# Four column groups of w_in as seven half-width products in a stage of their own

## The chip, the cores and the metric

The kernel runs on one core of a Trainium2 chip. The metric is the time of one execution in microseconds (us) on the device. The profiler takes one execution more, and the trace and its page are of that one.

## What is computed

One block of a network on x of 512 tokens by 2048 features, all in float32: a norm, the projection by `w_in`, eight heads of sparse attention (NSA, in two key groups) beside four heads of retention, the projection by `w_out`, and a feed-forward part with squared ReLU. Cut to what matters:

```python
h = rms_norm(x, norm_mix_pre)                       # 512 x 2048
proj = h @ w_in                                     # 2048 x 6680
q_a, kv_a, gate_a, q_r, k_r, v_r, g_r = split(proj) # 1024, 6*256, 24, then 4 times 1024
k_cmp = compress_kv(kv6[0], ...); v_cmp = compress_kv(kv6[1], ...)   # a small MLP over 31 windows of 32 tokens
gates = sigmoid(gate_a)
o_a = nsa_attention(q_a, k_cmp, v_cmp, kv6[2], ..., kv6[5], gates, t5_bias)
q_r, k_r = rope(q_r), rope(k_r)
o_r = silu(g_r) * retention(q_r, k_r, v_r)          # per head of 256, chunks of 128
mix = concat([o_a, o_r]) @ w_out
x = x + rms_norm(mix, norm_mix_post)
u = square(relu(rms_norm(x, norm_mlp_pre) @ w_up))  # 2048 x 8192
x = x + rms_norm(u @ w_down, norm_mlp_post)
```

With 512 tokens every block of keys is among the chosen and the window reaches over all of them, so the chosen keys and the window keys are each all keys up to the token.

## The kernel before, in words

**Products.** Each float32 product is three matmuls on rounded halves (`mm3`, L155 to L157): `split` (L141) makes the high half by an ACT cast (L143) and the low half by a DVE subtraction (L144). The normed and transposed x is kept as `Hh`, `Hl`. A weight *slab* is 256 rows of `w_in` by up to 512 columns (`Slab`, L168); SP's queue loads it into `raw`, `split` makes `whi`, `wlo`. A column group is eight slabs, one *block* of steps (B = 8). `feat_major` (L202) puts features on the partitions, `tok_major` (L224) tokens; both issue per slab 24 matmuls of the group's width (512 columns; 256 for v's second group), 192 to a group.

**Order.** `Driver` `drv` (L267) walks the steps: kv, k, q0 (512 columns each), v1 (256), then for each retention head `qk` and `vg` (512 each), with q1 behind head 0's. `Side` (L67) holds the units that run between: the bias table, two `compress` units, 16 `nsa_unit`s (group g, query tile i, pair of heads), four `ret_unit`s. A unit has a first part (scores) and a second (mixing, `outs`). A pump after each piece of a step (6 matmuls) lets one step of each part go: `two` at every second piece, `three` at three pieces of four, and `side.drain(units, firsts)` issues what is left until so many units are through. All of this is fixed when the program is made: each engine then takes its instructions in that order.

**The units' chains.** `nsa_unit`: scores on PE (L584), scaled and biased by DVE (L585), maxima (L603, L608), six exponentials on ACT (L612), a reciprocal and scalings on DVE (L616 to L622), four transposes per key tile (L647) whose results are split into `ph`, `pl`, and mixing matmuls into the bank `oT`, of which there is one. `ret_unit`'s `outs` (L713): for query tile i, i+1 matmuls into `oT` (L742), statistics by DVE (L744, L745, L161), a power by POOL (L162), two DVE passes (L748, L749), and the next tile's gate (ACT L717, DVE L718 to L720).

**The front.** x's norm and transposes run beside v0 with the gates (280 columns, `tok_outer`). Then the driver begins.

**After retention**: `w_out` (416 columns at a time, beside ret_unit 3), then up and down, which already use seven products for eight (`Feed`, from L893): of two halves of the rows and two of the columns, sums of weight quarters (DVE adds) times sums of x quarters, 256 columns to a matmul in up. These are left as they are.

Of the kernel before, what the change touches and what calls it, by code (L numbers as in the profile page):

```python
# [112 lines left out]
def block_kernel(ctx: ExitStack, tc: tile.TileContext, x, norm_mix_pre, w_in, cmp_pe_k, cmp_w1_k, cmp_b1_k,  # L113
# [54 lines left out]
    class Slab:  # L168
# [11 lines left out]
        def load(self):  # L180
# [4 lines left out]
            hi = pool.tile([P, KC, width], F32R, name="whi")  # L185
            lo = pool.tile([P, KC, width], F32R, name="wlo")
# [77 lines left out]

    side = Side()
# [36 lines left out]
    gw.tile([P, 16], F32, name="gap_w")  # L302
    wp = wctx.enter_context(tc.tile_pool(name="wp", bufs=3, side="right"))
    pool_a = lambda: (wp, S)
    actx, rctx = ExitStack(), ExitStack()
    ap = actx.enter_context(tc.tile_pool(name="att", bufs=1))


    def x_load(t, q):
        if q == 0:  # L310
            xts[t] = ap.tile([P, DM], F32, name="xt", tag="P", bufs=2)
# [4 lines left out]
    ones = ap.tile([1, P], F32, name="ones")  # L316
# [4 lines left out]
    g1 = ap.tile([1, DM], F32, name="g1", tag="P", bufs=2)  # L321
# [4 lines left out]
    gb = ap.tile([P, DM], F32, name="gb", tag="big")  # L326
# [15 lines left out]
    def x_square(t, q):  # L342
        if q == 0:
            hx[t] = ap.tile([P, DM if t % 2 else NG * 32 + DM], F32, name="h", tag="qT" if t % 2 else "kT")
            sx[t] = ap.tile([P, 8], F32, name="st", bufs=2)
        c = slice(q * 512, (q + 1) * 512)
        nc.scalar.activation(hx[t][:, c], xts[t][:, c], AF.Square, accum_out=sx[t][:, q:q + 1])
# [9 lines left out]
    Vh = ap.tile([P, NT, 2, NG * DK], F32R, name="Vh")  # L357
    Vl = ap.tile([P, NT, 2, NG * DK], F32R, name="Vl")
    gat = ap.tile([P, NT, 3 * HA], F32, name="gat")

    def v_done(b):
        def done(t, ps):
# [3 lines left out]
            split(Vh[:, t, b, :], Vl[:, t, b, :], ps[:, :NG * DK])  # L366
# [9 lines left out]
    ep = ectx.enter_context(tc.tile_pool(name="early", bufs=NSLAB))  # L376
    v0 = slabs_of(w_in, [(OFF_KV + 768, NG * DK), (OFF_GATE, 3 * HA)], lambda: (ep, NG * DK + 3 * HA))
    first = tok_outer(v0, NG * DK + 3 * HA, v_done(0))
    kv0 = slabs_of(w_in, [(OFF_KV, 512)], pool_a)
# [9 lines left out]
    for i in range(3, NSLAB):  # L389
        v0[i].fetch(wp.tile([P, KC, S], F32, name="raw", tag="whi" if i % 2 else "wlo"))  # L390
        if i in (3, 4):
            x_load(1, i - 1)
# [11 lines left out]
    for n in range(4 * NT):  # L404
# [20 lines left out]
        if n == 3:  # L425
            kv0[0].fetch()
            kv0[1].fetch()
        if n in (7, 11):
            kv0[n // 11].load()
# [4 lines left out]
    for _ in products:  # L434
        pass
    ectx.close()
    rp = rctx.enter_context(tc.tile_pool(name="ret", bufs=1, side="right", reuse_waits="tile"))

    hot = ap.tile([33, 640], F32, name="hot", tag="P", bufs=2)
    nc.gpsimd.dma_start(hot, c_hot)
    tbl = ap.tile([33, HA], F32, name="tbl")
    nc.vector.memset(tbl[32:33, :], NEG)
    nc.gpsimd.dma_start(tbl[0:32, :], t5_bias)
    g3r = ap.tile([KT, P], F32, name="g3r")
    nc.gpsimd.dma_start(g3r, norm_mlp_pre.rearrange("o (k p) -> (o k) p", p=P))
    rot = rp.tile([P, 2, S], F32, name="rot")
    nc.gpsimd.dma_start(rot, c_rot)
    RB = 16  # L450
    rd = dram.tile([HA, RB, RD], F32, name="rd")

    def bias_table():
        rsb = ap.tile([HA, 640], F32, name="rsb", tag="P", bufs=2)
        for c0, n in ((0, 512), (512, 128)):
            ps = bank("S")
            nc.tensor.matmul(ps[:HA, :n], tbl, hot[:, c0:c0 + n], start=True, stop=True)
            nc.vector.tensor_copy(rsb[:, c0:c0 + n], ps[:HA, :n])
            yield
        nc.gpsimd.dma_start(rd, rsb[:, None, :].to_broadcast([HA, RB, RD]))  # L460
        pt = bank("PT", 2)
        nc.tensor.transpose(pt[:, :KT], g3r, ident[:KT, :KT])
        nc.vector.tensor_copy(g3T, pt[:, :KT])
        yield

# [12 lines left out]
    def kv_done(f, ps):  # L478
        if f % 2 == 0:
            KV[f // 2] = ap.tile([P, NG * S + CBLK], F32, name="KV", tag="P", bufs=2)  # L480
        nc.scalar.copy(KV[f // 2][:, f % 2 * S:(f % 2 + 1) * S], ps)

    def compress(i):
        pe, w1, b1, w2 = ((cmp_pe_k, cmp_w1_k, cmp_b1_k, cmp_w2_k), (cmp_pe_v, cmp_w1_v, cmp_b1_v, cmp_w2_v))[i]
        kv = KV[i]
        pes = ap.tile([CBLK, DK], F32, name="pes")
        nc.sync.dma_start(pes, pe[0])
        b1s = ap.tile([DK, 2], F32, name="b1s")
        nc.sync.dma_start(b1s[:, 0:1], b1.rearrange("o n -> n o"))
        w2s = ap.tile([DK, DK], F32, name="w2s")  # L490
        nc.sync.dma_start(w2s, w2[0])
        w1s = [ap.tile([P, 16, DK], F32, name="w1s", tag=("qT", "big")[c]) for c in range(2)]
        for c in range(2):
            nc.sync.dma_start(w1s[c], w1[0][c * 16 * P:(c + 1) * 16 * P, :].rearrange("(l p) n -> p l n", p=P))
            yield
# [5 lines left out]
        for l in range(CBLK):  # L501
            nc.tensor.matmul(hid[:65, :DK], kv[:, l:l + STRIDE * 64 + 1:STRIDE], w1s[l // 16][:, l % 16, :],  # L502
                             start=l == 0, stop=l == CBLK - 1)
            if l % 8 == 7:
                yield
        hs = ap.tile([65, DK], F32, name="hs")
        nc.scalar.copy(hs, hid[:65, :DK])
        yield
# [3 lines left out]
        z = ap.tile([DK, 4, 63], F32, name="z")  # L512
# [25 lines left out]
    def k_done(f, ps):  # L538
        nc.scalar.copy(kW[:, f % 2, :] if f // 2 else kS[:, f % 2, 32:], ps)

    def q_done(g):
        def done(f, ps):
            if f == 0:
                QT[g] = ap.tile([P, 4, S], F32, name="qT", tag="qT")
            nc.scalar.copy(QT[g][:, f, :], ps)
        return done
# [10 lines left out]
    def nsa_unit(g, i, pr):  # L557
# [7 lines left out]
        def scores():  # L565
# [196 lines left out]
    def proj(cols, done, tok=False):  # L762
        sl = slabs_of(w_in, cols, pool_a)
# [783 lines left out]
```

## Time and profile before

| what | us |
|---|---|
| three timed runs: median (lowest to highest) | 2201.61 (2201.35 to 2202.2) |
| the profiled execution: its time, its span | 2200.95, 2199.0 |
| PE busy, of 12787 matmul rows | 2154.7 (98%) |
| PEld (weight loads) | 1910.5 (87%) |
| DVE | 1535.1 (70%) |
| ACT | 984.4 (45%) |
| POOL | 122.7 (6%) |
| mean granted TensorE clock | 0.994 |

The busy time of PE is the sum of modelled spans that overlap; how fast it goes is read from the start of one matmul to the start of the next. Share of the chain that ended last: PE 90%, DVE 5%, the rest 1% each or less.

### The profile page before, as it was taken

The page shows a single profiled execution, that of the slowest core. Times are in us where ns is not written, and L with a number is a line of the kernel's source. Part 1 is how long each engine was busy: PE and PEld are TensorE (multiplying, and loading weights), DVE is VectorE, ACT ScalarE, POOL GpSimd, SP SyncE. Part 2 cuts the span into 40 slices and gives each one's busy share as a digit, 9 for nine tenths or more (in the row PEclk, how much of TensorE's full clock was granted, in tenths as well). Part 3 has the DMA queues.
Part 4 walks back from the last instruction along what each step waited for, and adds up shares of the span by engine and source line. Part 5 has one row for each costly group of instructions (what it writes and reads, how often), then busy time and mean ns, then how long its engine had stood idle before and what let it go on. Part 6 is the DMA issues. An engine that isn't in the chain of part 4 may idle for free.

```text
span 2199.0 us, 31984 instructions
## 1 busy us (share of the span) xinstructions
PE 2154.7 (98%) x12787; PEld 1910.5 (87%) x12787; DVE 1535.1 (70%) x1828; ACT 984.4 (45%) x1425; POOL 122.7 (6%) x139
## 2 busy tenths in 40 slices
PE   8999999999999999999999999999999999999995
PEld 7888878878788899999999999999888888888874
DVE  6213555554555533578988877777878999999996
ACT  5213343343232323485554555555664454445453
POOL 0000000000000000000000000000000000000011
PEclk9999999999999999999999999999999999999997
DMA  6543324322324334577877757676775757566684
GB/s 198 135 120 90 94 65 96 94 75 82 86 75 124 109 101 129 176 233 214 230 218 205 207 165 204 168 205 184 235 230 166 213 157 224 145 202 185 189 220 99
DMA packets 255462, 348.97 MB, mean 159 GB/s; under 512 B 16299, under 2 KB 166139, under 8 KB 254417
## 3 DMA queue, kind: packets, MB, share of 16 engines
q1 hardware_dynamic: 199472, 263.07, 38.0%
q0 software_dynamic: 29616, 42.96, 11.8%
q10 hardware_dynamic: 26226, 40.91, 5.1%
q8 instruction: 100, 1.64, 0.3%
q14 instruction: 48, 0.39, 0.1%
HBM read 305.14 MB, written 41.75 MB: 158 GB/s over the span
## 4 chain that ended last, share of the span: by engine, by line
PE 90%; DVE 5%; issue 1%; ACT 1%; DMA 1%; POOL 0%; SPq 0%; DVEq 0%; ACTq 0%; POOLq 0%
PE prod L157 17%; PE prod L155 17%; PE prod L156 17%; PE mm L155 11%; PE mm L157 11%; PE mm L156 11%; PE S L584 2%; DVE wlo L938 2%; PE PT L647 1%; PE S L707 1%; PE oT L742 1%; PE oT L502 1%; PE oT L155 1%; PE oT L156 1%; PE oT L157 1%
## 5 line engine op out<-in xcount | busy, mean ns | idle before, releaser
L961 ACT CAST whi<-Y 128x1024 fp32r<-128x1024 f32 x227 | 238.2, 1050 | 283.1 <-PE prod L157 117.6
L156 PE MATMUL prod<-wlo,Hh 128*128 128x512 f32 x896 | 349.4, 390 | 2.3 <-DVE wlo L938 2.1
L157 PE MATMUL prod<-whi,Hl 128*128 128x512 f32 x896 | 348.7, 389 | 0.0
L155 PE MATMUL prod<-whi,Hh 128*128 128x512 f32 x896 | 348.6, 389 | 0.0
L144 DVE TENSOR_TENSOR wlo<-raw,whi 128x1024 fp32r<-128x1024 f32 (+4 forms) x152 | 168.6, 1113 | 255.1 <-ACT whi L143 254.6
L961 ACT CAST whi<-low 128x1024 fp32r<-128x1024 f32 x215 | 226.4, 1054 | 265.1 <-PE prod L157 131.6
L938 DVE TENSOR_TENSOR wlo<-Y,whi 128x1024 fp32r<-128x1024 f32 x227 | 276.8, 1220 | 51.5 <-ACT whi L961 50.5
L938 DVE TENSOR_TENSOR wlo<-low,whi 128x1024 fp32r<-128x1024 f32 x215 | 262.1, 1221 | 55.9 <-ACT whi L961 55.0
L157 PE MATMUL prod<-Hh,wlo 128*128 128x256 f32 x1024 | 284.3, 278 | 5.1 <-DVE wlo L938 5.1
L155 PE MATMUL prod<-Hh,whi 128*128 128x256 f32 x1024 | 284.6, 278 | 0.3 <-ACT Hh L143 0.3
L156 PE MATMUL prod<-Hl,whi 128*128 128x256 f32 x1024 | 284.0, 277 | 0.9 <-DVE Hl L144 0.9
L143 ACT CAST whi<-raw 128x1024 fp32r<-128x1024 f32 (+4 forms) x152 | 145.6, 960 | 302.0 <-PE mm L156 147.9
L155 PE MATMUL mm<-whi,Hh 128*128 128x416 f32 (+4 forms) x704 | 262.3, 373 | 0.6 <-ACT Hh L143 0.5
L157 PE MATMUL mm<-whi,Hl 128*128 128x416 f32 (+4 forms) x704 | 248.1, 352 | 0.7 <-DVE Hl L144 0.7
L156 PE MATMUL mm<-wlo,Hh 128*128 128x416 f32 (+4 forms) x704 | 247.6, 352 | 0.0
L155 PE MATMUL mm<-Hh,whi 128*128 128x512 f32 x512 | 214.7, 419 | 0.1
L155 PE MATMUL prod<-sx,whi 128*128 128x256 f32 x768 | 212.0, 276 | 0.0
L156 PE MATMUL prod<-sx,whi 128*128 128x256 f32 x768 | 212.0, 276 | 0.0
L157 PE MATMUL prod<-sx,wlo 128*128 128x256 f32 x768 | 212.0, 276 | 0.0
L156 PEld LDWEIGHTS prod<-wlo,Hh 128*128 128x128 f32 x896 | 168.2, 188 | 40.1 <-DVE wlo L938 5.3
L157 PE MATMUL mm<-Hh,wlo 128*128 128x512 f32 x512 | 200.5, 392 | 0.0
L156 PE MATMUL mm<-Hl,whi 128*128 128x512 f32 x512 | 200.0, 391 | 0.0
(273 smaller groups left out, 3909.4 us busy)
## 6 DMA issues: line engine op xcount, KB each, us to landing
raw<-in_w_in SPq DMA_DIRECT2D x160, 256.0 KB, 3.1
low<-in_w_up SPq DMA_DIRECT2D x76, 512.0 KB, 4.3
Y<-in_w_up SPq DMA_DIRECT2D x64, 512.0 KB, 4.7
low<-in_w_down SPq DMA_DIRECT2D x64, 512.0 KB, 4.6
Y<-in_w_down SPq DMA_DIRECT2D x64, 512.0 KB, 4.6
Y<-ud SPq DMA_DIRECT2D x49, 512.0 KB, 8.0
ud<-Y ACTq DMA_DIRECT2D x77, 256.0 KB, 4.8
raw<-in_w_out SPq DMA_DIRECT2D x32, 416.0 KB, 3.5
```

The source lines that it names most:

```text
L143: nc.scalar.copy(hi, src)
L144: nc.vector.tensor_sub(lo, src, hi.bitcast(F32))
L155: nc.tensor.matmul(ps, ah, bh, start=first, stop=False, skip_group_check=more)
L156: nc.tensor.matmul(ps, ah, bl, start=False, stop=False, skip_group_check=more)
L157: nc.tensor.matmul(ps, al, bh, start=False, stop=last, skip_group_check=more)
L502: nc.tensor.matmul(hid[:65, :DK], kv[:, l:l + STRIDE * 64 + 1:STRIDE], w1s[l // 16][:, l % 16, :], start=l == 0, stop=l == CBLK - 1)
L584: nc.tensor.matmul(sps[:, :c + L], QT[g][:, h, qs], k, start=True, stop=True)
L647: nc.tensor.transpose(pt[:, e * P:(e + 1) * P], Pt[:, e, rows_of(j)], ident)
L707: nc.tensor.matmul(sps[:, :n], QK[:, 2 + d, rows_of(j)], QK[:, d, j * P:], start=d == 0, stop=d == 1)
L742: nc.tensor.matmul(o[:, :DR], AT[:, a0:a0 + P], vr[:, j, :], start=j == 0, stop=j == i)
L938: nc.vector.tensor_sub(lo, src, hi.bitcast(F32))
L961: nc.scalar.copy(hi, src)
```

## The change

Four groups of 512 columns (kv, k, q0, q1: `INC`) are no longer products of 512 columns under the driver. They are made by `groups()` in a stage of their own between v and retention: for each group seven products of 48 matmuls of 256 columns, 336 in all, where 192 of 512 columns stood; the scheme is that of up. `Feed` and `Later` are moved up and take their pool and place as arguments. The steps:

- v1 is the driver's first block. Beside it, `in_sums()` makes the four sums of x quarters that the products need (28 DVE operations of 128x1024, 8 ACT casts; each second piece of a step, and later each second piece of `groups()`). Three weight operands are made (`ifeed.advance()`) two steps before v1 ends.
- `in_done` takes a product's bank to `z[0]`, `z[1]` by ACT or DVE; ACT's queue stores them to `pd` in DRAM (512 KB each). v's halves go to `vd` in DRAM by POOL's queue; v1's results lie two to a buffer (`vst`).
- POOL's queue loads them back, and the compressor's weights: kv and the first compressor's at the end of `groups()`, the second's during the first compressor, V (2 MB) at the second's middle, then k, the bias `BT` (8 transfers), q0; q1 later.
- The bias table is made in one piece behind v0's products; its three loads are issued by POOL at n == 9 of x's norm.
- The eight retention blocks are now blocks 2 to 9 of the driver (v1 is the first); side units go beside the first seven. ret 0 stands ahead of i = 2 of group 0, ret 2 ahead of i = 2 of group 1; `every` pumps after each piece.

```diff
-    kv0 = slabs_of(w_in, [(OFF_KV, 512)], pool_a)
+    first = tok_outer(v0, NG * DK + 3 * HA, v_done(0, lambda: xp.tile([P, S], F32R, name='vst')))
+    v1 = slabs_of(w_in, [(OFF_KV + 1280, 256)], pool_a)
...
     def v_done(b, vst):
-            split(Vh[:, t, b, :], Vl[:, t, b, :], ps[:, :NG * DK])
+            v = vst().rearrange("p (a n) -> p a n", a=2)
+            split(v[:, 0, :], v[:, 1, :], ps[:, :NG * DK])
+            nc.gpsimd.dma_start(vd[:, :, t, b, :].rearrange("a p n -> p a n"), v)
...
+    INC = [(OFF_KV, OFF_KV + 256), (OFF_KV + 512, OFF_KV + 1024), (0, 256), (512, 768)]
...
+    def groups():
+        for i, (g, p, _) in enumerate(iphases):
...
+                ps = mm.tile([P, S], F32, name="mm")
...
+            for s in range(2):
+                hi, lo = ifeed.slab()
+                if s == 0 and sets:
+                    in_done(*sets.pop())
...
+                for f in range(2):
+                    for kk in range(4):
+                        k = 4 * s + kk
+                        o = ps[:, f * 256:(f + 1) * 256]
...
+                        mm3(o, hi[:, kk, rows_of(f)], lo[:, kk, rows_of(f)], xh[:, k, :], xl[:, k, :], start, last,
+                            more)
+                    yield
...
+    drv.steps += tok_major(v1, 256, v_done(1, vst))
+    work = in_sums()
+    sums = lambda c: next(work, None) if c % 2 else None
...
+    drv.run(len(drv.steps) - 2, pump=sums)
+    raws = [wr.tile([P, KC, S], F32, name="raw").rearrange("p k n -> p (k n)") for _ in range(3)]
+    ifeed.free += raws
+    for _ in range(3):
+        ifeed.advance()
+    drv.run(len(drv.steps) - 1, pump=sums)
+    drv.run()
+    next_up = slabs_of(w_in, [(OFF_QR, DR), (OFF_KR, DR)], pool_a)
+    for n, _ in enumerate(groups()):
+        if n % 2 or n % 8 == 0:
+            next(work, None)
...
-            nc.sync.dma_start(w1s[c], w1[0][c * 16 * P:(c + 1) * 16 * P, :].rearrange("(l p) n -> p l n", p=P))
+            nc.gpsimd.dma_start(w1s[c], w1[0][c * 16 * P:(c + 1) * 16 * P, :].rearrange("(l p) n -> p l n", p=P))
...
+    def loads():
+        k_load()
+        load_bias(0)
+        q_load(0)
+        for _ in range(6):
+            yield
...
+    side.add(lambda: compress(0), nothing)
+    side.add(lambda: compress(1), nothing)
+    side.add(loads, nothing)
     for u in range(8):
-        side.add(*nsa_unit(0, u // 2, u % 2), after(3), after(4))
-    side.add(*ret_unit(0), after(6))
+        if u == 4:
+            side.add(*ret_unit(0), after(2), after(3))
+        side.add(*nsa_unit(0, u // 2, u % 2))
+    side.add(*ret_unit(1), after(4), after(5))
     for u in range(8):
-        side.add(*nsa_unit(1, u // 2, u % 2), after(7))
-        if u == 5:
-            side.add(*ret_unit(1), after(9))
-    side.add(*ret_unit(2), after(10), after(11))
-    side.add(*ret_unit(3), after(12))
-    for blocks, units, firsts, pump in ((3, 3, 0, two), (4, 0, 0, two), (7, 10, 11, three), (8, 11, 12, three),
-                                        (9, 12, 12, three), (10, 12, 19, two), (11, 19, 19, two),
-                                        (12, 22, 22, three)):
+        if u == 4:
+            side.add(*ret_unit(2), after(6), after(7))
+        side.add(*nsa_unit(1, u // 2, u % 2))
+    side.add(*ret_unit(3), after(8))
+    kv_load()
+    compress_load(0)
+    for blocks, units, firsts, pump in ((2, 0, 0, every), (3, 0, 0, three), (4, 7, 8, three), (5, 8, 0, three),
+                                        (6, 12, 13, three), (7, 13, 0, three), (8, 22, 22, every)):
         drv.run(blocks * B - 1, pump=pump)
         side.drain(units, firsts)
```

**Where v1 ends and the groups begin, ACT, in the changed kernel** (`half_`: a loaded quarter of weights; `sv_`: a sum of x quarters; `da`: a result; L143 splits `whi` and `vst`, L362 is the cast in `Feed.advance`, L656 the one in `in_sums`):

```order
L143 CAST whi<-raw 128x2x256 x4
L656 CAST sv_613<-db 128x1024 x2
L143 CAST whi<-raw 128x2x256 x2
L362 CAST whi<-half_621 128x1024
L362 CAST whi<-half_622 128x1024
L362 CAST whi<-half_623 128x1024
L656 CAST sv_617<-db 128x1024 x2
L143 CAST vst<-mm 128x256 x4
L362 CAST whi<-half_624 128x1024
L362 CAST whi<-half_625 128x1024
L681 COPY da<-mm 128x2x256
```

And DVE at the same place:

```order
L339 TENSOR_TENSOR wlo<-half_621,whi 128x1024
L339 TENSOR_TENSOR wlo<-half_622,whi 128x1024
L658 TENSOR_TENSOR sv_618<-db,sv_617 128x1024 x2
L144 TENSOR_TENSOR vst<-mm,vst 128x256 x4
L644 TENSOR_TENSOR db<-db,Hh 128x1024 x2
```

The third weight cast and the two of a sum stand ahead of v1's casts on ACT, and the sum's two subtractions ahead of v1's on DVE; none of these rows is in the kernel before.

**The outs of retention head 2, DVE, before** (`rst` statistics, `rn` the normed result, `sg`, `gr` the gate):

```order
L719 RECIPROCAL sg<-sg 128x256
L720 TENSOR_TENSOR gr<-gr,sg 128x256
L144 TENSOR_TENSOR wlo<-raw,whi 128x1024
L744 BN_STATS rst<-oT 128x6
L745 BN_AGGR rst<-rst 128x2
L161 TENSOR_SCALAR rst<-rst 128x1
L748 TENSOR_SCALAR rn<-oT,rst 128x256
L749 TENSOR_TENSOR rn<-rn,gr 128x256
```

and in the changed kernel, where these lines are L1040 to L1071:

```order
L1041 RECIPROCAL sg<-sg 128x256
L1042 TENSOR_TENSOR gr<-gr,sg 128x256
L1066 BN_STATS rst<-oT 128x6
L1067 BN_AGGR rst<-rst 128x2
L161 TENSOR_SCALAR rst<-rst 128x1
L1070 TENSOR_SCALAR rn<-oT,rst 128x256
L1071 TENSOR_TENSOR rn<-rn,gr 128x256
L144 TENSOR_TENSOR wlo<-raw,whi 128x1024
```

A `wlo` is one slab, 24 main matmuls. On PE 18, 12 and 18 main matmuls stand between the four tiles' `oT` matmuls before, and 12, 12 and 12 in the changed kernel; for head 0 it is 12, 18, 18 before and 18, 18, 12 now, for head 1 24 each before and 18, 12, 18 now.

**The end of the last nsa unit, DVE, before:**

```order
L608 TENSOR_REDUCE nst<-Pt 128x2
L144 TENSOR_TENSOR pl<-PT,ph 31x256
L144 TENSOR_TENSOR wlo<-raw,whi 128x1024 x2
L616 RECIPROCAL nst<-nst 128x6
L618 TENSOR_TENSOR nst<-nst,gat 128x6
L622 TENSOR_SCALAR Pt<-Pt,nst 128x512 x4
L622 TENSOR_SCALAR Pc<-Pc,nst 128x31 x2
L690 TENSOR_TENSOR rt<-QK,rot 128x512
```

and in the changed kernel:

```order
L930 TENSOR_REDUCE nst<-Pt 128x2
L144 TENSOR_TENSOR pl<-PT,ph 31x256
L938 RECIPROCAL nst<-nst 128x6
L940 TENSOR_TENSOR nst<-nst,gat 128x6
L944 TENSOR_SCALAR Pt<-Pt,nst 128x512 x4
L944 TENSOR_SCALAR Pc<-Pc,nst 128x31 x2
L144 TENSOR_TENSOR pl<-PT,ph 128x512 x4
L144 TENSOR_TENSOR pl<-PT,ph 31x256
L144 TENSOR_TENSOR wlo<-raw,whi 128x1024 x2
```

The unit now ends inside `drain(22, 22)`, with no main matmul and no slab between its scores and its end.

## Rows read from the trace of the kernel before

**Rows 1.** The page: span, and busy time of each engine.

```profile
span 2199.0 us, 31984 instructions
PE 2154.7 (98%) x12787; PEld 1910.5 (87%) x12787; DVE 1535.1 (70%) x1828; ACT 984.4 (45%) x1425; POOL 122.7 (6%) x139
```

**Rows 2.** PE's waits from 0 to 960 us: line, releaser, us in total, times, longest.

```profile
PE oT L742 <- DVE rn L748: 0.7, 1, 0.7
```

**Rows 3.** Timeline of PE at 180 us, 512 columns: start, us, instruction.

```profile
179.74 0.39 PE L156 MATMUL mm<-Hl,whi 128*128 128x512 f32 x1
179.96 0.39 PE L157 MATMUL mm<-Hh,wlo 128*128 128x512 f32 x1
```

**Rows 4.** Windows in up: PE, PEld, DVE, ACT, POOL busy; clock; DMA share; GB/s.

```profile
1100.00:1150.00 50.00, 50.00 (x442) 50.00 (x441) 41.32 (x42) 27.27 (x33) 2.54 (x2) 1.00 0.74 211
```

**Rows 5.** The page's groups: a weight load beside 512 columns.

```profile
L156 PEld LDWEIGHTS prod<-wlo,Hh 128*128 128x128 f32 x896 | 168.2, 188 | 40.1 <-DVE wlo L938 5.3
```

**Rows 6.** Timeline of PE where side work breaks in.

```profile
562.01 0.40 PE L157 MATMUL mm<-Hh,wlo 128*128 128x512 f32 x1
562.25 0.61 PE L707 MATMUL S<-QK 128*128 128x128 f32 x4
562.61 0.48 PE L155 MATMUL mm<-Hh,whi 128*128 128x512 f32 x1
562.93 0.40 PE L156 MATMUL mm<-Hl,whi 128*128 128x512 f32 x1
```

**Rows 7.** Timeline of PE at the driver's first products.

```profile
51.60 1.02 PE L457 MATMUL S<-hot,tbl 33*8 33x512 f32 x2
52.55 0.50 PE L155 MATMUL mm<-Hh,whi 128*128 128x512 f32 x1
```

**Rows 8.** Groups by form, 50 to 760 us, DVE and ACT: busy, mean ns | idle.

```profile
L144 DVE TENSOR_TENSOR wlo<-raw,whi 128x1024 fp32r<-128x1024 f32 x94 | 114.9, 1222 | 168.5 <-ACT whi L143 168.4
L144 DVE TENSOR_TENSOR pl<-PT,ph 128x512 fp32r<-128x512 f32 x40 | 27.7, 692 | 56.8 <-ACT ph L143 56.7
L144 DVE TENSOR_TENSOR Vl<-mm,Vh 128x256 fp32r<-128x256 f32 x4 | 1.4, 414 | 0.0
...
L143 ACT CAST whi<-raw 128x1024 fp32r<-128x1024 f32 x94 | 98.5, 1048 | 203.2 <-PE mm L156 138.6 <-DMA raw<-in_w_in 18.9 <-DVE Hl L144 15.8
```

**Rows 9.** Timeline, outs of retention head 0: DVE's pass that frees `oT`.

```profile
394.76 0.54 DVE L748 TENSOR_SCALAR rn<-oT,rst 128x256 f32<-128x256 f32 x1 [0.67 <-POOL rst L162]
...
400.82 0.54 DVE L748 TENSOR_SCALAR rn<-oT,rst 128x256 f32<-128x256 f32 x1 [0.73 <-POOL rst L162]
```

**Rows 10.** Timeline, an nsa unit of i = 3 from its last score to its transposes.

```profile
338.79 1.02 PE L584 MATMUL S<-kT,qT 128*128 128x512 f32 x2
...
340.93 1.22 DVE L608 TENSOR_REDUCE nst<-Pt 128x2 f32<-128x1024 f32 x1
...
343.80 0.32 ACT L612 ACTIVATE Pc<-Pc,nst 128x31 f32<-128x31 f32 x1
...
347.15 0.18 ACT L612 ACTIVATION_READ_ACCUMULATOR Pt<-Pt,nst 128x1 f32 x1
...
349.87 1.67 DVE L622 TENSOR_SCALAR Pt<-Pt,nst 128x512 f32<-128x512 f32 x4
...
351.66 0.60 PE L647 MATMUL PT<-misc,Pt 128*128 128x128 f32 x4
```

**Rows 11.** Windows of PE behind a wait: us, PE busy, clock, DMA share, GB/s.

```profile
990.00:994.00 4.00, 0.39 (x4) 1.00 1.01 323
994.00:995.00 1.00, 0.79 (x6) 1.00 0.73 271
995.00:999.00 4.00, 4.00 (x23) 0.57 0.90 197
```

**Rows 12.** Windows with `w1s` on SP's queue, and with `BT` on POOL's (columns of rows 4).

```profile
160.00:172.00 12.00, 12.00 (x56) 9.45 (x54) 3.50 (x10) 1.90 (x4) 3.98 (x8) 1.00 0.89 173
136.00:148.00 12.00, 12.00 (x61) 9.95 (x60) 1.74 (x2) 2.73 (x5) 0.00 (x0) 1.00 1.04 332
```

More of the change, by code (lines that the diff above doesn't have):

```diff
@@ L265, in block_kernel, with __init__, add, step @@
+    class Later:
+        def __init__(self):
+            self.at, self.todo = 0, []
+        def add(self, slabs, work):
+            self.todo.append((self.at + slabs, work))
+        def step(self):
+            self.at += 1
+            due = [w for n, w in self.todo if n <= self.at]
+            self.todo = [(n, w) for n, w in self.todo if n > self.at]
+            for w in due:
+                w()
     side = Side()
@@ L435, in block_kernel @@
         pass
+    bias_table()
     ectx.close()
[L437 to L447 removed]
+    xctx.close()
@@ new lines, in in_sums, with part, less, more_of @@
+    def in_sums():
+        add, sub = nc.vector.tensor_add, nc.vector.tensor_sub
+        def part(h, i, c):
+            k0 = 8 * h + 4 * c
+            return tuple(H[:, k0:k0 + 4, i * 256:(i + 1) * 256] for H in (Hh, Hl))
+        def less(v, a, b):
+            sub(v, a[0].bitcast(F32), b[0].bitcast(F32))
+            yield
+            add(v, v, a[1].bitcast(F32))
+            yield
+            sub(v, v, b[1].bitcast(F32))
+            yield
+        def more_of(v, f, a):
+            for x in a:
+                f(v, v, x.bitcast(F32))
+                yield
+        def both(p, make):
+            works = [make(c) for c in range(2)]
+            while next(works[0], "end") != "end":
+                yield
+                next(works[1])
+                yield
+            his = [tuple(H[:, 4 * c:4 * c + 4, :] for H in IA[p]) for c in range(2)]
+            for c in range(2):
+                nc.scalar.copy(his[c][0], vs[c])
+            for c in range(2):
+                sub(his[c][1], vs[c], his[c][0].bitcast(F32))
+                yield
+        vs = [ip.tile([P, SL], F32, name="db", bufs=2).rearrange("p (k n) -> p k n", k=4) for _ in range(2)]
+        yield from both(2, lambda c: less(vs[c], part(0, 1, c), part(1, 1, c)))
+        yield from both(4, lambda c: more_of(vs[c], sub, part(0, 0, c)))
+        yield from both(5, lambda c: more_of(vs[c], add, part(1, 0, c)))
+        yield from both(3, lambda c: less(vs[c], part(0, 0, c), part(0, 1, c)))
@@ new lines, in block_kernel @@
+    ifeed.free += raws
+    for _ in range(3):
+        ifeed.advance()
[5 more added lines that the diff above has]
+            next(work, None)
+        if raws and not ifeed.loads and all(any(r is f for f in ifeed.free) for r in raws):
+            for i in range(3):
+                next_up[i].fetch()
+            raws = []
+        if ifeed.at == 2 * len(iphases) and not hasattr(next_up[0], "hi"):
+            next_up[0].load()
@@ L448, in block_kernel @@
+    assert not raws
+    ictx.close()
+    ap = actx.enter_context(tc.tile_pool(name="att", bufs=1, reuse_waits="tile"))
+    rp = rctx.enter_context(tc.tile_pool(name="ret", bufs=1, side="right", reuse_waits="tile"))
     rot = rp.tile([P, 2, S], F32, name="rot")
     nc.gpsimd.dma_start(rot, c_rot)
[L450 to L464, printed above, removed]
@@ L1128, in block_kernel @@
     phases += [(("down", c, nb), p, dn_source(c, nb)) for c in range(NCH) for nb in range(2) for p in ORDER]
-    feed = Feed(phases, [low0, low1], 3, [("down", NCH - 1, nb) for nb in range(2)])
+    feed = Feed(phases, halved(low0) + halved(low1), 3, [("down", NCH - 1, nb) for nb in range(2)], hp,
+                lambda g, p, s: 40 if isinstance(g, int) and p == 6 and s else 0)
     tmp = Ring(*xt, *(xh[:, c:c + 512] for c in range(0, 2048, 512)))
```

404 lines of the change are left out of this document (248 added, 156 removed).

## The prediction

> **What bounds the kernel now.** I read the page first: PE is busy for 98% of the span, DVE 70%, ACT 45% [rows 1]. PE takes its instructions in order, so the list of its waits came next: in the first 960 us the units cost it next to nothing; the only wait on a retention unit is 0.7 us [rows 2]. Then the timeline gives what a matmul costs, start to start, since the modelled spans overlap: 0.2267 us at 512 columns (the 0.22 to 0.23 between neighbours of [rows 3] agree) and, in up, 442 matmuls of 256 columns in 50 us, 0.1131, say 0.1133, half of it [rows 4]. So time goes where PE's matmuls go, or where PE begins to wait. The profiled execution took 2200.95 us, 0.03% under the median of 2201.61; my sum stands on the former.
>
> **What the change takes away.** (1) Products: 4 x 192 = 768 matmuls of 512 columns go, 174.1 us; 4 x 336 = 1344 of 256 columns come, 152.3 us: **-21.8**. (2) Side work that breaks into the main matmuls costs more than its columns: four matmuls of 128 columns, 0.23 us by the same pace, lie in 0.92 us with two of 512, which need 0.45, so 0.24 goes at the seam [rows 6]. The listed order has 198 such seams before and 183 after: **-3.0** at 0.2. Together -24.8, and this much is nearly certain if PE keeps its pace.
>
> In separate sentences: the Trainium skill's page "TensorE: Matmul & The Clock Gate", section "Back-to-back issue gap", has sustained spacings set by weight load and matmul together, 81 ns at 128 columns and 131 at 512. A straight line between them gives an estimate of 98 ns at 256, and the exchange would then cost +31 us instead of saving 22. The trace differs, with 227 and 113 ns.
>
> **What it adds: waits of PE.** The groups need DVE for some 26 of 38 us each by the durations of [rows 8], less than its share in up (41.3 of 50, where PE was full [rows 4]), so in their middle I take no loss. Five places remain.
>
> (3) *Front.* v1's 192 matmuls of 256 columns end some 21.8 us after they start near 53.0 (where the first products start now [rows 7]), at 74.8. The third weight cast waits for the last of them (its buffer) and takes 1.05 [rows 8]; behind it on ACT stand two sum casts, on DVE the two subtractions they feed, then v1's four casts and subtractions. The sum's subtractions run from about 76.9 to 79.1 and v1's first (0.41) ends at 79.5; only then is a bank free for the groups' first product. PE waits **4.7 us**. After a wait of 3.8 us PE's granted clock fell to 0.57 over 4 us, its level of 1.2 GHz, and PE gave 23 matmuls where 35 fit at 0.1133 [rows 4, 11]: **+1.4** more. Bounds: 0, if the third cast finds a free buffer earlier, to 8.
>
> (4) *Loads by POOL.* kv and the first compressor's weights are asked for about 8 us before the groups end, and a 1 MB `w1s` pair moved at 332 GB/s [rows 12], so they cost nothing; without that cover 6 us. V, k, BT, q0 (2, 1, 1, 1 MB) follow each other on POOL's queue in the second compressor; BT alone moved at 173 GB/s, with slabs beside it [rows 12]. At the faster rate 4 MB take 13 us and BT 6, about 19; 60 main matmuls (13.6 us) and some 5 us of units cover them. Taken **+0.5**, between 0 and 11 (all 5 MB at 173 GB/s, 29 us).
>
> (5) *Retention's outs.* `oT` is one bank, and DVE frees it every 6.1 us where a slab's subtraction lies between, 4.9 without [rows 9]. PE has, per tile, 12 or 18 main matmuls (2.7 or 4.1 us), its own one to four and two transposes. With 18 it keeps up, which is why only 0.7 us shows before. Head 2 now has 12, 12, 12 and the gate's exponential stands behind an nsa unit's on ACT: **+5.8** (bounds 2 to 7). Head 0 with 18, 18, 12 beside the scores of i = 2, whose DVE work stands in the same chain: **+2.4** (0 to 4). Head 1 with 18, 12, 18: **+1.3** (0.7, as the same spacing cost before, to 3).
>
> (6) *Change of unit under `every`.* Its transposes come 12 matmuls earlier than DVE has scaled `Pt`: two places, **+1.4** (0 to 3).
>
> (7) *The drain.* From the last score of an i = 3 unit it took 3.4 us to the end of the maxima; the exponentials took 3.5 and the scaling 1.7 [rows 10]. In between lay slab work that the drain has not; with some 0.2 of small steps the chain is 8.8. PE has in this time the score itself (0.9), fifteen matmuls of 256 columns (1.7) and two transposes (0.3): 5.9 idle. Then the first key tile needs a cast and a subtraction, 1.3 together (the second is 0.69 of it [rows 8]), of which a transpose set (0.44, four of the shape in [rows 10]) covers part: 0.9. The steps before the last score miss their main matmuls too, 0.5. In all **+7.3** beside 12.6 us of PE's own work (4 to 11, the upper with the clock falling as in [rows 11]).
>
> Bias table: its matmuls stand before v1 instead of inside the blocks, the same number, and their loads are issued some 15 us earlier; nothing. Stores of v and of the groups ride queues with nothing behind them that PE needs; nothing, up to 1 us.
>
> **Sum**: -24.8 + 6.1 + 0.5 + 9.5 + 1.4 + 7.3 = 0.0, so 2201.0 us; I say **2201**. It is a difference of two large numbers. The first is firm, the second is a chain of estimates, each possibly half.
>
> **Rivals.** A measurement here tells 0.2% (4.4 us) from no change.
>
> *A, faster: the waits are short.* Before, head 0 (12, 18, 18) and head 2 (18, 12, 18) lay at nearly these spacings and PE waited 0.7 us in all [rows 2], so (5) and (6) may come to 2 instead of 10.9, and if the front loses no clock step and the drain costs its lower bound, 3.3 and 1.4 more go. 2201 - 8.9 - 4.7 = 2187; with (5) and (6) alone 2192. For it: PE's units before hid almost everything. Against it: the rows of the changed order show less main work at just these places.
>
> *B, slower: POOL's queue is late.* Place: the first nsa scores, behind V, k, BT and q0 on one queue. Price: 11 us more at BT's rate throughout, 2212. It decides once q0 lands later than some 19 us after V is asked for. For it: 173 against 332 GB/s [rows 12], and a DMA share of 0.9 already without V. Against: BT comes in eight transfers of short rows, while V, k and q are one or two long ones each.
>
> In sentences of their own: the Trainium skill's "SBUF — State Buffer" (its box on the "DVE blocks DMA" trap) says that POOL's DMAs get no descriptors while DVE holds the port they share in its faster float32 modes. By that rule B would be more likely, since DVE works beside the compressors. In the window with BT on POOL's queue DVE was busy for 3.5 of 12 us only, so the trace here does not settle it.
>
> *C, slower: pairs are paced by their weight loads.* If two half-width pairs cost more than one full one in this stage, at worst 0.188 each as a load beside 512 columns shows [rows 5], 1344 cost 252.7 instead of 152.3: up to +100, 2301. It decides above 0.13 us a pair, where the saving is gone. [Rows 4] speak against it: 441 loads in 50 us, at full pace. By the page on TensorE named above it would be 2254 with the other terms kept.
>
> **How the numbers follow.** Forecast, 2197 to 2205: 0.38. A, and what lies between: 0.34. B, with a front or drain at its upper bound counted to it: 0.26. C: 0.02. The likeliest case's own range is 2197 to 2205. For 8 in 10 I take in A down to 2188 and B up to 2212, leaving out the rest of both and C. Faster by over 0.2% is 0.34, within 0.38, slower 0.28.
>
> **What would show it.** Right: in the groups, 442 matmuls of 256 columns per 50 us; PE idle 4 to 5 us behind v1, released by DVE, and a clock of 0.5 behind it; PE waits on `rn` of 5 us in the last block of units; 7 us of waits on `Pt`, `ph` and `pl` at the end of the units. Wrong: a first nsa score that waits on a DMA (B); DVE at 100% in the groups with PE waiting on `wlo`; waits of under 10 us in sum (A).

## The result and the profile after

The changed kernel takes 2220.64 us (median of 4 runs, 2218.67 to 2221.53) where the one before takes 2201.9 in the same comparison: a ratio of 1.0084, 95% interval 1.0066 to 1.0101. It is 18.7 us slower; the forecast was 2201 with 2188 to 2212. The profiled execution took 2221.53. Its page:

```profile
span 2219.8 us, 33410 instructions
PE 2151.1 (97%) x13363; PEld 1930.6 (87%) x13363; DVE 1634.2 (74%) x1924; ACT 1013.5 (46%) x1453; POOL 152.5 (7%) x175
```

Against [rows 1] PE has 576 matmuls more and is busy for 3.6 us less, in a span that is 20.8 us longer. So the time went into PE's waits, or into a slower PE. PE's list of waits, 0 to 700 us, which had one entry of 0.7 for these units in [rows 2]:

```profile
PE mm L155 <- DVE vst L144: 4.8, 1, 4.8
PE oT L1064 <- DVE rn L1070: 4.6, 3, 2.8
PE oT L813 <- ACT KV L809: 4.1, 1, 4.1
...
```

the drain's own, 670 to 735 us:

```profile
PE PT L969 <- DVE Pt L944: 2.5, 1, 2.5
PE oT L156 <- DVE pl L144: 1.3, 2, 1.0
```

and, as windows with the columns of [rows 4], the waits (of the front, the first compressor, head 2's outs and the drain), what follows each, and one undisturbed window of the groups (120 to 140):

```profile
72.60:77.40 4.80, 0.07 (x1) 0.00 (x0) 4.35 (x6) 4.03 (x7) 0.00 (x0) 0.90 0.65 191
77.50:83.20 5.70, 5.70 (x27) 5.70 (x28) 5.45 (x7) 0.41 (x1) 2.84 (x4) 0.50 0.91 224
120.00:140.00 20.00, 20.00 (x179) 20.00 (x178) 15.99 (x17) 8.24 (x9) 1.95 (x2) 1.00 0.60 175
229.00:239.00 10.00, 10.00 (x72) 9.31 (x71) 4.04 (x6) 2.10 (x2) 4.07 (x6) 1.00 0.93 317
239.00:249.00 10.00, 6.11 (x27) 4.44 (x25) 1.23 (x1) 2.02 (x3) 1.64 (x3) 0.91 1.05 337
249.00:254.00 5.00, 4.79 (x20) 4.50 (x21) 1.23 (x1) 0.16 (x2) 0.00 (x0) 0.50 0.65 189
627.00:630.00 3.00, 0.21 (x1) 0.00 (x0) 2.15 (x6) 0.42 (x1) 0.55 (x1) 0.91 0.49 165
630.00:636.00 6.00, 5.94 (x15) 4.70 (x16) 5.06 (x11) 1.74 (x3) 0.54 (x1) 0.50 0.08 22
698.00:701.00 3.00, 0.53 (x3) 0.17 (x3) 1.30 (x5) 1.85 (x7) 0.00 (x0) 1.00 0.06 19
701.00:708.00 7.00, 6.86 (x28) 5.87 (x29) 3.10 (x7) 1.76 (x3) 0.00 (x0) 0.51 0.03 10
```

The window of the groups shows the pace that the change counts on: 179 matmuls of 256 columns in 20 us. The others come in pairs: a stretch in which PE stands, and behind it one with a granted clock of 0.50, TensorE's level of 1.2 GHz. In the front's, 27 matmuls take 5.7 us, where 50 or 51 fit at the pace of the groups. PE is called busy there all the same; only the clock column and the counts show the loss.

To place the whole difference I took, for each PE matmul of both traces, the time to the next one's start. At 0.2267 and 0.1133 us for 512 and 256 columns (and the usual spacing of other widths) the main matmuls need 21.8 us less than before. The steps into and out of side work cost 2.3 us less. All the rest, waits, half clock and the side instructions held up by either, is 43.9 us more (with 1.0 us at the ends of the span, that is the 20.8). By stretch, I summed each step less the median of the same step in the kernel before; the table gives this less the same sum of the kernel before over those times. A row can miss by one or two us, and the rows come to 40.8 of the 43.9:

| stretch of the changed kernel | forecast | measured |
|---|---|---|
| v1's end and first groups (55 to 100 us) | 6.1 | 8.0 |
| rest of the groups | 0 | 0.9 |
| kv and weights for the first compressor (225 to 275) | 0 | 6.4 |
| first scores behind POOL's loads | 0.5 | 0.2 |
| head 0's outs and the nsa unit beside | 2.4 | 4.7 |
| head 1's | 1.3 | 0.6 |
| head 2's, change of unit | 7.2 | 6.1 |
| the drain (670 to 730) | 7.3 | 9.6 |
| turn from up to down (1570 to 1620) | 0 | 4.3 |

The last is no part of the change's path: ACT waits there 4.0 us for a load of `xh`, 1.1 in the kernel before, and in the profiles of the twelve kernels below the same stretch costs 0.8 at most. Why it happened in this execution wasn't tried. So a single run of a variant is read by its stretches, not by its time against 2220.6 alone.

### The profile page after: what moved, and what is told of

The parts are those of the page before. It is cut to its first block, busy times and chain, and to the rows that moved or that the text cites. A ratio compares the mean times of both kernels' runs of the same rounds, so it can differ in the third digit from the quotient of the medians.

```text
span 2219.8 us, 33410 instructions
## 1 busy us (share of the span) xinstructions
PE 2151.1 (97%) x13363; PEld 1930.6 (87%) x13363; DVE 1634.2 (74%) x1924; ACT 1013.5 (46%) x1453; POOL 152.5 (7%) x175
## 4 chain that ended last, share of the span: by engine, by line
PE 84%; DVE 8%; DMA 3%; ACT 2%; issue 2%; POOL 0%; SPq 0%; ACTq 0%; DVEq 0%; POOLq 0%
PE prod L157 16%; PE prod L156 16%; PE prod L155 16%; PE mm L155 10%; PE mm L157 10%; PE mm L156 10%; DVE wlo L339 2%; PE S L905 2%; DMA raw<-in_w_in 2%; PE PT L969 1%; PE S L1029 1%; PE oT L813 1%; PE oT L1064 1%; DMA xh<-ud 1%; PE oT L155 1%
## 5 line engine op out<-in xcount | busy, mean ns | idle before, releaser
L362 ACT CAST whi<-Y 128x1024 fp32r<-128x1024 f32 x227 | 238.2, 1050 | 285.6 <-PE prod L157 121.2
L362 ACT CAST whi<-low 128x1024 fp32r<-128x1024 f32 x215 | 226.3, 1054 | 265.7 <-PE prod L157 132.7
L144 DVE TENSOR_TENSOR wlo<-raw,whi 128x1024 fp32r<-128x1024 f32 (+4 forms) x120 | 129.3, 1083 | 163.3 <-ACT whi L143 162.9
L143 ACT CAST whi<-raw 128x1024 fp32r<-128x1024 f32 (+4 forms) x120 | 111.8, 936 | 206.1 <-PE mm L157 100.4
L155 PEld LDWEIGHTS prod<-whi,Hh 128*128 128x128 f32 x896 | 168.6, 188 | 36.3 <-ACT whi L362 1.3
L157 PEld LDWEIGHTS prod<-whi,Hl 128*128 128x128 f32 x896 | 168.5, 188 | 34.8
L157 PEld LDWEIGHTS prod<-Hh,wlo 128*128 128x128 f32 x1024 | 193.0, 188 | 5.6 <-DVE wlo L339 5.6
```

The source lines that it names most:

```text
L143: nc.scalar.copy(hi, src)
L144: nc.vector.tensor_sub(lo, src, hi.bitcast(F32))
L155: nc.tensor.matmul(ps, ah, bh, start=first, stop=False, skip_group_check=more)
L157: nc.tensor.matmul(ps, al, bh, start=False, stop=last, skip_group_check=more)
L362: nc.scalar.copy(hi, src)
```

## The experiments

All are the changed kernel with the edit shown, one execution each but for the last two; the kernel before ran beside each set, at 2201.1 to 2203.6 us. What a stretch "costs" here is its time over the usual steps, without the subtraction of the table: 8.1 for the front, 7.3 for kv, 4.5 for head 0, 6.9 for head 2 and 10.7 for the drain in the changed kernel.

**1. One weight operand fewer ahead of v1's end.**

```diff
-    for _ in range(3):
+    for _ in range(2):
         ifeed.advance()
```

> The changed kernel with two weight operands made ahead of v1's end instead of three. Theory (order of ACT's and DVE's queues): the third weight cast, which waits for v1's last product, no longer stands ahead of v1's casts, so PE's wait behind v1 (4.97 us start to start over a normal step) falls under 1.5 and the 6.8 us at a granted clock of 0.5 behind it go: 2220.6 less 6 to 8, about 2213. Rival (DVE is simply late with the sums, whatever stands ahead): the wait stays at 4 to 5 us and the time within 1.5 us of 2220.6.

Measured: 2215.97. The stretch goes from 8.1 over normal pace to 5.4, the wait to 3.0. Half right, as the timeline of this run (start, us, instruction) shows. First the changed kernel:

```profile
72.70 1.04 ACT L362 CAST whi<-half 128x1024 fp32r<-128x1024 f32 x1 [1.80 <-PE mm L157]
73.65 1.99 ACT L656 CAST sv<-db 128x1024 fp32r<-128x1024 f32 x2
74.72 2.36 DVE L658 TENSOR_TENSOR sv<-db,sv 128x1024 fp32r<-128x1024 f32 x2 [0.45 <-ACT sv L656]
75.55 1.18 ACT L143 CAST vst<-mm 128x256 fp32r<-128x256 f32 x4
77.00 1.41 DVE L144 TENSOR_TENSOR vst<-mm,vst 128x256 fp32r<-128x256 f32 x4
77.48 0.58 PE L155 MATMUL mm<-Hh,whi 128*128 128x256 f32 x1 [4.81 <-DVE vst L144]
```

and with two casts:

```profile
73.07 1.18 ACT L143 CAST vst<-mm 128x256 fp32r<-128x256 f32 x4
73.14 2.35 DVE L658 TENSOR_TENSOR sv<-db,sv 128x1024 fp32r<-128x1024 f32 x2
...
75.42 1.40 DVE L144 TENSOR_TENSOR vst<-mm,vst 128x256 fp32r<-128x256 f32 x4
75.88 0.39 PE L155 MATMUL mm<-Hh,whi 128*128 128x256 f32 x1 [3.04 <-DVE vst L144]
```

ACT's cast of v1 now comes as soon as v1 is there, but on DVE the two subtractions of a sum still stand ahead of v1's.

**2. The same wait, filled with matmuls nobody reads.**

```diff
+    fill = bank("S")
+    for _ in range(20):
+        nc.tensor.matmul(fill, Hh[:, 0, rows_of(0)], Hh[:, 0, :], start=True, stop=True)
     next_up = slabs_of(w_in, [(OFF_QR, DR), (OFF_KR, DR)], pool_a)
```

> The changed kernel with 20 matmuls of 512 columns (4.5 us by the usual pace) put on PE between v1 and the groups, whose result nothing reads. Theory (a wait also costs the granted clock behind it): the products begin when they did before, since the wait is only filled, but the clock stays at 1.0, and some 3 us of half pace go: 2217 to 2218. Rival (the half clock costs nothing, since the groups wait for DVE there anyway): the time stays within 1 us of 2220.6. Third (the fill delays the products itself): 2 us or more slower.

Measured: 2214.81; 0.991 mean clock for 0.987. The windows of this run, over the same times:

```profile
72.60:77.40 4.80, 4.53 (x21) 3.43 (x19) 4.32 (x6) 4.00 (x7) 0.00 (x0) 1.00 0.66 196
77.50:83.20 5.70, 5.70 (x51) 5.70 (x52) 5.70 (x8) 1.26 (x2) 2.84 (x4) 1.00 0.87 210
```

The products begin when they did (77.35 for 77.48), DVE and ACT have the same load up to there, and 51 matmuls stand where 27 stood: 24 x 0.1133 = 2.7 us, which is the clock alone. So the front's 8 us are a wait of 5 and a clock of some 3; the half clock does cost, and the fill delays nothing. The rest of the 5.8 us in time is the turn to down and, by 1.3 us, the drain, which this edit leaves as it was (15.5 us for 16.8 from the start of the last score to that of the last mixing matmul). Its clock happened to be down for half as long (0.97 in the mean from 670 to 730 us, 0.94 in the changed kernel).

**3. No sums beside v1's last two steps, and two casts.**

```diff
-    for _ in range(3):
+    for _ in range(2):
         ifeed.advance()
-    drv.run(len(drv.steps) - 1, pump=sums)
+    drv.run(len(drv.steps) - 1)
```

> The changed kernel with two weight operands made ahead instead of three, and no piece of the sums beside v1's last two steps. Theory (with two casts 3.2 us of wait were left because two sum subtractions of 1.2 us stood ahead of v1's on DVE): PE's wait behind v1 falls under 1 us and the half clock behind it goes, 6 to 8 us less there; the sums come later, so PE's waits on the low halves of weights in the groups (2.0 us now) may grow by up to 2. 2211 to 2215. Rival (DVE's whole load in v1 and the first groups is too much, and the wait only moves): the same sum of waits to 120 us, 2218 or more.

Measured: 2211.77. The stretch costs 1.3 for 8.1, the rest of the groups 2.0 as before, and PE's wait of this name is

```profile
PE mm L155 <- DVE vst L144: 0.8, 1, 0.8
```

So the front's loss is what stands ahead of v1's results on ACT and on DVE, and the sums have room enough later. Some 4 us of the time gained are the turn to down, which costs 0.8 at most in each of these runs.

**4. The first compressor one piece earlier.**

```diff
-        for _ in range(2 if i else 5):
+        for _ in range(2 if i else 4):
```

> The changed kernel with the first compressor one piece (6 main matmuls, 1.4 us) earlier. Theory (the copy of the position rows stands on ACT behind the cast of a weight slab that lands late): the copy now stands ahead of that cast, PE waits only until the first half of the compressor's weights has landed, near 245 to 246, so 2 to 4 us of the 4.3 go and perhaps the half clock behind it (2.4): 2214 to 2218. Rival (PE waits for the compressor's weights themselves, late on POOL's queue): PE waits to about 249 as before, 2220 to 2221.

Measured: 2222.03, and PE's wait grew to 5.8, ending at 249.2 as before. That looks like the rival, but the edit was a miss: on ACT the copy still stands behind the same cast, as the listed order of both shows. So it tells nothing between the two; experiment 7 makes the edit properly.

**5 and 6. The first compressor three pieces later; rot's load later.**

```diff
-        for _ in range(2 if i else 5):
+        for _ in range(2 if i else 8):
```

> The changed kernel with the first compressor three pieces (18 main matmuls, 4.1 us) later. Theory (the compressor's weights land near 248 because every DMA engine is busy from 229 to 249 us with rot, kv, the weights, two stores and the slabs): the wait of 4.3 us falls under 0.7, the half clock behind it (2.4) goes; the pieces come out of the 36 main matmuls that stand unpumped ahead of head 2's outs, so the drain does not grow. 6 to 7 us less, 2212 to 2215. Rival (a slab waited for on ACT is what PE waits for): the wait stays above 3 us.

```diff
-    nc.gpsimd.dma_start(rot, c_rot)
...
         q_load(0)
+        nc.gpsimd.dma_start(rot, c_rot)
```

> The changed kernel with the 512 KB load of rot behind q0's instead of ahead of kv's. Theory (bytes in flight delay the compressor's weights): 0.5 MB less at some 320 GB/s, the wait of 4.3 us shrinks by 1.0 to 2.2, the clock behind it may or may not fall; 2216 to 2219. Rival (the latency of POOL's queue, not the bytes): less than 0.7 of change.

Measured: 2213.47 and 2212.58. The stretch (7.3) falls to 3.0 and 3.2, the clock stays up in both, and PE's wait, 4.1 before, is 1.5 with the first and with the second

```profile
PE oT L812 <- ACT KV L808: 2.2, 1, 2.2
```

Experiment 5 expected a wait under 0.7, so that is half a miss: 1.5 us stay, and the time came into its range with the turn to down. In experiment 6 half a MB in another place, which nothing needs for 100 us, gave 1.9 us of wait and 2 of clock. DMA issues from 225 to 262 us in the changed kernel (KB each, us to landing):

```profile
raw<-in_w_in SPq DMA_DIRECT2D x12, 256.0 KB, 9.3
w1s<-in_cmp_w_k POOLq DMA_DIRECT2D x2, 1024.0 KB, 14.1
```

and with rot later, over the same times:

```profile
raw<-in_w_in SPq DMA_DIRECT2D x12, 256.0 KB, 8.0
w1s<-in_cmp_w_k POOLq DMA_DIRECT2D x2, 1024.0 KB, 11.8
```

Over the whole of the changed kernel a slab takes 3.1 us. With the windows at 229 to 249 us (317 and 337 GB/s, DMA share 0.93 and 1.05) this reads as a queue of bytes: rot, kv, 2 MB of weights, two stores and the slabs share the DMA engines. No run separates the bytes from rot's place ahead of kv and the weights on POOL's own queue; that SP's slabs land sooner too speaks for the bytes.

**7. The first compressor two pieces earlier: the copy ahead of the cast.**

```diff
-        for _ in range(2 if i else 5):
+        for _ in range(2 if i else 3):
```

> The changed kernel with the first compressor two pieces earlier, so that the copy of the position rows stands on ACT ahead of the weight slab's cast that waits until 248 us (one piece earlier had left ACT's order as it was). Theory (PE waits for the copy behind that cast, not for the compressor's weights): the copy comes behind the cast before it, near 245, and PE's first compressor matmul starts there, 4 us earlier than 249.2; it may wait again for the second half of the weights. Rival (the compressor's weights on POOL's queue): the first compressor matmul stays at 248.5 or later, with a wait of some 7 us.

Measured: 2216.55. In the changed kernel, at the first compressor:

```profile
243.75 1.05 ACT L143 CAST whi<-raw 128x1024 fp32r<-128x1024 f32 x1 [6.28 <-DMA raw<-in_w_in]
...
248.03 1.04 ACT L143 CAST whi<-raw 128x1024 fp32r<-128x1024 f32 x1 [3.23 <-DMA raw<-in_w_in]
248.98 0.18 ACT L809 COPY KV<-PT 128x32 f32<-128x32 f32 x1
...
249.21 1.12 PE L813 MATMUL oT<-w1s,KV 128*65 128x128 f32 x4 [4.10 <-ACT KV L809]
```

and with the copy ahead of the second of these casts:

```profile
244.71 1.04 ACT L143 CAST whi<-raw 128x1024 fp32r<-128x1024 f32 x1 [7.19 <-DMA raw<-in_w_in]
245.66 0.18 ACT L809 COPY KV<-PT 128x32 f32<-128x32 f32 x1
...
245.89 2.79 PE L813 MATMUL oT<-w1s,KV 128*65 128x128 f32 x16 [3.46 <-ACT KV L809]
```

PE starts 3.3 us earlier, so it waited for a small copy that stood behind a cast whose slab was late, and not for the compressor's weights. The stretch still costs 6.9: PE comes sooner too, and waits behind the first late slab instead of the second. What is late is the slabs; what turns it into PE's wait is the order on ACT.

**8. The drain behind the last step.**

```diff
-        drv.run(blocks * B - 1, pump=pump)
+        drv.run(blocks * B - (blocks < 8), pump=pump)
         side.drain(units, firsts)
```

> The changed kernel with the last step of the last block of units pumped too and the drain behind it instead of ahead of it: 24 main matmuls more stand between the last units' pieces. Theory (the drain costs PE's waits for want of main matmuls): of the 10.1 us over normal pace in the drain 3 to 5 go: 2215 to 2218. Rival (the drain's waits come from DVE being behind, not from too little main work): within 1.5 us of 2220.6.

Measured: 2213.59. The drain costs 8.8 for 10.7; the rest of the gain is mostly the turn to down. That is less than expected: there are four pieces more with main matmuls, but the wait for the last unit's scaling is still there (2.3 for 2.5). And the 1.9 us are not shown to be the added matmuls: the clock is down for half as long here (0.97 from 670 to 730 us), as in experiment 2, where an unchanged drain was 1.3 us shorter with it.

This run shows something else at head 2, which its edit leaves alone. Its `oT` matmuls in the changed kernel:

```profile
623.86 0.60 PE L1064 MATMUL oT<-vr,AT 128*128 128x256 f32 x2
630.06 2.08 PE L1064 MATMUL oT<-vr,AT 128*128 128x256 f32 x4 [2.85 <-DVE rn L1070]
636.93 1.46 PE L1064 MATMUL oT<-vr,AT 128*128 128x256 f32 x6
641.20 1.89 PE L1064 MATMUL oT<-vr,AT 128*128 128x256 f32 x8
```

and in this run:

```profile
622.32 0.60 PE L1064 MATMUL oT<-vr,AT 128*128 128x256 f32 x2
628.51 1.13 PE L1064 MATMUL oT<-vr,AT 128*128 128x256 f32 x4 [2.85 <-DVE rn L1070]
633.44 1.56 PE L1064 MATMUL oT<-vr,AT 128*128 128x256 f32 x6 [0.82 <-DVE rn L1070]
639.50 1.99 PE L1064 MATMUL oT<-vr,AT 128*128 128x256 f32 x8 [1.53 <-DVE rn L1070]
```

The same first wait, and the clock stays at 1.00 here (600 to 670 us; 0.95 in the changed kernel). PE waits 5.2 us in sum instead of 2.8, but from the first to the last of these rows it is 17.2 us against 17.3. So at head 2 the half clock costs next to nothing: what PE loses by it, it would have waited for DVE.

**9. Head 2's unit last, and the drain behind the last step.**

```diff
-        if u == 4:
-            side.add(*ret_unit(2), after(6), after(7))
         side.add(*nsa_unit(1, u // 2, u % 2))
+    side.add(*ret_unit(2), after(6), after(7))
...
-        drv.run(blocks * B - 1, pump=pump)
+        drv.run(blocks * B - (blocks < 8), pump=pump)
```

> The changed kernel with head 2's unit behind the nsa units and the drain behind the last step, so that no main matmul passes without a piece beside it where one is wanted. Theory (the drain's 10.1 us over normal pace and its clock come from units without main matmuls): under 2 are left there, while head 2's outs, still 12 main matmuls apart, keep 4 to 7. 2220.6 less 8 to 10: 2210 to 2213. Rival (DVE's and ACT's work in these blocks is the bound wherever it stands): less than 4 us of gain.

Measured: 2205.83, some 4 us of it the turn to down. Head 2 and the drain together cost 7.2 for 17.6, all of it now head 2's outs:

```profile
PE oT L1064 <- DVE rn L1070: 3.8, 4, 1.7
PE PT L1047 <- DVE rn L1071: 1.6, 1, 1.6
```

With an edit in two places that is the sum of both; experiment 8 alone gave 1.9 of the 10.4. Where head 2 stood it held back the nsa units behind it until its v was there (36 main matmuls pass without a piece), and they were then drained.

**10. 18 main matmuls between head 2's tiles, and nothing else.**

```diff
                 held = (i, n)
                 yield
+                if h == 2:
+                    yield
```

> The changed kernel with 18 main matmuls instead of 12 between the tiles of head 2, and nothing else. Theory (12 are too few for a chain of 4.9 us or more on DVE; and what is pumped later is drained without main matmuls): the 6.9 us over normal pace at head 2 fall by 2.5 to 5, the drain's 10.7 grow by 3 to 6: within 2.5 us of the changed kernel. Rival (the gate's exponential behind the nsa unit's on ACT, not the spacing, sets the wait): head 2 loses less than 1.5.

Measured: 2221.09. Head 2 costs 3.0 for 6.9 and the drain 15.1 for 10.7: both as expected. The spacing is what head 2 waits for, and the room for it has to come from somewhere.

**11 and 12. All of it together.** Edits 3, 6, 8, 9 and 10, the compressor one piece later (6 for 5), and `every` in the seventh block too; then also the spacing for heads 0 and 1 (`h < 3`) and `every` in the sixth.

> The changed kernel with all of it together: two casts and no sums beside v1's last two steps, rot behind q0, the first compressor one piece later, head 2 behind the nsa units with 18 main matmuls between its tiles, every piece pumped in the last two blocks of units, the drain behind the last step. Theory (the loss is the sum of these five waits and the granted clock behind each, and each can be had back by itself): front 6.8, kv 4 to 6, drain and head 2 together 12 to 15 of their 17.6 go; 2192 to 2197, faster than before (2201.4) by 0.2 to 0.4%. Rival (what is mended at one place comes back as a wait at the next, since DVE and ACT have the same work): 2203 or more.

> As the one with all of it together, with the wider spacing for heads 0 and 1 too, and every piece pumped in the block before as well to make room. Theory (the 4.5 and 2.4 us over normal pace at heads 0 and 1 come from 12 and 18 main matmuls between tiles that need DVE for 4.9 to 6.1 us): 2 to 4 us less than that one, 2189 to 2194. Rival (their waits come from the nsa scores of the same stretch on DVE): within 1.5 us of it.

Measured: 2196.77 us (10 runs, 2193.08 to 2198.81), a ratio to the kernel before of 0.9972, interval 0.9962 to 0.9982; and 2195.08 (5 runs), 0.997, interval 0.9957 to 0.9983. Both are faster than either kernel, by 0.3% against the one before; the two are not told apart. The first lies within what was expected, the second a little above. PE's waits from 60 to 720 us in the first:

```profile
PE oT L1063 <- DVE rn L1069: 2.2, 2, 1.3
PE PT L840 <- DVE z L836: 2.2, 1, 2.2
PE mm L157 <- DVE wlo L339: 1.1, 2, 0.8
PE S L904 <- DVE Pt L905: 1.0, 1, 1.0
PE mm L155 <- DVE vst L144: 0.8, 1, 0.8
PE oT L812 <- ACT KV L808: 0.7, 1, 0.7
```

None is longer than 2.2 us, and in this execution the clock does not fall in these stages. The stretches: front 1.4, kv 3.8, head 0 3.8, head 2 and drain 3.3. In the second, head 0 falls to 2.0 as expected, but kv costs 6.0 (its clock fell once there), so the wider spacing shows no gain in sum that is clear of the spread.

## Why the prediction was wrong

The steps that held: (1), 21.8 us off the products, and (2), 2.3 us for the 3.0 of the seams. Rival C (pairs paced by weight loads) is out: 179 pairs in 20 us. Rival B (V, k, BT and q0 late at the first scores) did not happen: 0.2 us there. Rival A is out too. What the change adds in waits, clock and held-up side work was 44 us where I had 25. Of these 19, the table places 6.4 at kv, 4.3 at the turn to down, 2.3 at head 0, 2.3 in the drain and 1.9 in the front; heads 1 and 2 came out 1.8 below, and some 3 are not placed. The waits alone, as PE's list has them from 60 to 730 us, come to some 22, near the 23.4 that I had without a clock term; but 4.1 of them stand at kv, where I had none, with fewer in the drain and at head 2. Two steps of the prediction failed.

- **Step (4), kv and the first compressor's weights "cost nothing".** They cost 6.4. I set their 3 MB against a rate of 332 GB/s, which in [rows 12] was that of all queues together, at a DMA share of 1.04 (the second line; the heading names the two windows in the other order). I left out what moves with them: rot, two stores, and the slabs that PE needs next. It all moved at about that rate, and took 20 us. I had priced the case ("without that cover 6 us") but kept it out of the range, and looked for the late load at the wrong place, the nsa scores. Nor did PE wait for these loads themselves: they made SP's slabs late (9.3 us for 3.1), ACT stood at a slab's cast, and a copy of 0.18 us behind it held PE (experiments 6 and 7).
- **The clock.** I counted 1.4 us, in step (3) alone, and only as an upper bound in (7). It fell behind four of the waits. In the front it cost 2.7 us (experiment 2, and the counts 27 and 51); at kv about 2, which are part of the 6.4 (experiment 6); in the drain 1.3 for half of its stretch (experiment 2), so some 2 to 3 in all by estimate; at head 2 next to nothing (experiment 8). That is about 7 us where 1.4 stood. [Rows 11] had the price. I used it for the wait of 4.7 us and for none of the others.

By size: step (3), the wait itself, was 4.7 and measured 4.8, by the order that I gave, and experiment 3 shows that order to be all of it. Steps (5) and (6) at head 2: 7.2, with 6.1 measured. Where the clock stays up, its waits on `rn` are 5.2 (experiment 8) for the 5.8 of step (5), so DVE's chain was rightly priced; experiment 10 shows the spacing as its cause. Head 0 was 2.4 and measured 4.7; experiment 12's wider spacing gave back 2 us there, and where the rest comes from was not tested. Step (7), the drain: 7.3 for 9.6, but not as I had it: PE waits 3.8 us in the list where I had 5.9 of idle time, and the rest is the clock and short gaps. That the sum came near is partly luck. Experiment 9 shows that the drain came from the place of head 2's unit, which my working did not see.

The 4.3 us at the turn to down, known from the profiled execution alone, stay open.

The two rules of the Trainium skill that I weighed: for "TensorE: Matmul & The Clock Gate" (section "Back-to-back issue gap") the trace after differs as the one before did, 0.112 us for 256 columns where its two figures give an estimate of 0.098. For the "DVE blocks DMA" box of "SBUF — State Buffer" no run here shows it: the late loads of the changed kernel moved at 317 to 337 GB/s with DVE busy for 40% and 12% of the two windows, and as far as the runs show, what delayed them went with the bytes in flight.

## What to carry to other kernels

Where engines take their work in order, a saving on PE is worth what is left after each engine's queue has been read past the places that the change moves: ask for every result PE needs next what stands ahead of it on ACT and DVE, and whether that thing itself waits for something (a buffer, a late load). Add to the price of a wait of PE like these (2.5 to 4.8 us) up to 2 to 3 us for the clock that may fall behind it, and next to nothing where another engine sets the pace there, as DVE did at head 2. And sum the bytes of all queues in a stretch, not those of the new loads alone. A change that loses by waits need not be undone: here moving a few things took away or shortened most of the waits, and the same products then gained 0.3%.

## What the runs showed of the hardware

- PE's granted clock fell to 0.50 behind waits shorter than the 3.8 us that had shown it before: 2.8 (head 2) and 2.5 (the drain) in the changed kernel. The wait alone does not tell: behind the same 2.8 us at head 2 it stayed at 1.00 in experiments 6 and 8. Behind a wait of 2.2 us for `z` it stayed at 1.00 in experiment 11 and was 0.51 over the next 3.5 us in experiment 12, and in experiment 10 it fell behind one of 1.4 among short side steps. What decides between them stays open. Filling the front's wait of 4.8 us with matmuls kept it at 1.00.
- With SP's and POOL's loads and ACT's stores in flight at once the transfers ran at 317 to 337 GB/s in sum, and each paid: a 256 KB slab 9.3 us for 3.1, a 1 MB weight load 14.1 us. Moving 0.5 MB away took 1.3 us off the slabs and 2.3 off the weights.
- The half clock cost 2.7 us in 5.7 in the front, where PE set the pace, and 0.2 in 17.3 at head 2, where PE waits for DVE at either level.
